# Lp-pooling on one core: a second small piece of 840 columns on partitions 30 to 89, loaded behind the first large load and stored on SP, with more implied waits declared away

## The chip, the cores and the metric

One core of one Trainium2 chip. Times are device microseconds of a whole execution of the kernel; "span" is the part of it that the profile covers, from the first to the last instruction.

A word on names. The profile counts sixteen DMA engines. A transfer over all 128 partitions is split over the sixteen (eight packets each; those of the first large load land at 19.63 to 20.34 us in the kernel before). I call one such engine with its packets a **ring**. q1 is the queue that SP issues to (all 2,432 load packets of 52,736 bytes are in it in the kernel before), q10 the one of ACT, ScalarE's sequencer (with the 896 packets of the seven ACT stores). Where both hold packets a ring takes from both: the sixteenth ran stores of 26,368 bytes and loads of 52,736 by turns from 75.04 to 86.72 us. ACT also stands for ScalarE, DVE for VectorE.

## The reference

```python
x: (32, 256, 4096) float32, p = 2.0, kernel_size = 4
for i in range(1024):
    window = np.abs(x[:, :, 4*i:4*i+4]) ** p
    result[:, :, i] = np.mean(window, axis=-1) ** (1.0 / p)
```

With p = 2 that is the root of the mean of four squares: 134.22 MB are read and 33.55 MB written, with very little arithmetic on each number.

## The kernel before

The input is treated as one flat array, 262,144 columns on 128 partitions. It is cut into 20 big loads, most of 13,184 columns (6.75 MB), which turn through three SBUF slots. For each: ScalarE squares in place, VectorE sums groups of four into an output tile, ScalarE takes the root, and the tile is stored.

```python
slots = [[(W, [W])]] * 17 + [[(W, [6592, 6592])]]                       # load widths and chunks
slots += [[(W, [5792, 7392])], [(10808, [6592, 2808, 1408])]]
ODD = 840                                                              # columns of the small piece
...
Q = 30
odd = ODD * P // Q
t = o_tiles[1][0:Q, 0:odd]                                             # 30 rows of 3,584 columns
nc.sync.dma_start(out=t, in_=...)                                      # first of all transfers
while ahead < n and loads[ahead][0] < X_SLOTS:
    load(ahead)                                                        # three big loads, on SP
    ahead += 1
nc.vector.tensor_tensor(out=t, in0=t, in1=t, op=mult)                  # the small piece: square,
nc.vector.tensor_reduce(out=o, in_=..., op=add)                        # sum,
nc.scalar.activation(out=o, in_=o, func=Sqrt, scale=1.0 / k)           # root,
stores["odd"] = nc.scalar.dma_start(...)                               # store on ACT
...
follows(ins, before)   # declares: ins needs no wait of its own on these, another wait implies it
```

Seven of the big stores are issued by ACT, the last four by SP.

Of the kernel before, what the change touches and what calls it, by code (L numbers as in the profile page):

```python
# [8 lines left out]
@with_exitstack  # L9
def kernel(  # L10
    ctx: ExitStack,
    tc: tile.TileContext,
    x: bass.AP,
    p: float,
    kernel_size: int,
    out: bass.AP,
):

    nc = tc.nc

    assert float(p) == 2.0, "kernel specialized for p == 2"
    k = int(kernel_size)
    assert k == 4, "kernel specialized for kernel_size == 4"  # L30

    P = nc.NUM_PARTITIONS
    fp32 = mybir.dt.float32
    Act = mybir.ActivationFunctionType
    xf = x.rearrange("b c l -> (b c l)")
    of = out.rearrange("b c l -> (b c l)")
    total = xf.shape[0] // P

    W, O_W = 13184, 6592
    X_SLOTS, O_SLOTS = 3, 2  # L40
    slots = [[(W, [W])]] * 17 + [[(W, [6592, 6592])]]
    slots += [[(W, [5792, 7392])], [(10808, [6592, 2808, 1408])]]
    ODD = 840
    groups = [2] * 9 + [1, 1]
    late = {7, 8, 9, 10}
    in_x = {9: (2, 0), 10: (2, 3296)}
    FINE, ENDS, LAGS = {19}, {18}, {8: 2}
    PAIRS = 15
    ON_DVE = {(18, 0)}

    loads = [(s, sum(w for w, _ in slot[:j]), *slot[j]) for s, slot in enumerate(slots)
             for j in range(len(slot))]
    n = len(loads)
    assert sum(w for _, _, w, _ in loads) + ODD == total

    firsts = [sum(groups[:g]) for g in range(len(groups))]
    assert sum(groups) == n
    group_of = [g for g, count in enumerate(groups) for _ in range(count)]
    columns = [sum(w for _, _, w, _ in loads[firsts[g]:firsts[g] + groups[g]])  # L60
               for g in range(len(groups))]

    x_pool = ctx.enter_context(tc.tile_pool(name="x_pool", bufs=1))
    o_pool = ctx.enter_context(tc.tile_pool(name="o_pool", bufs=1))

    x_tiles = [x_pool.tile([P, W], fp32, name=f"xt{j}") for j in range(X_SLOTS)]
    o_tiles = [o_pool.tile([P, O_W], fp32, name=f"ot{j}") for j in range(O_SLOTS)]
    ctx.enter_context(tc.manual_schedule())

    def block(flat, g, div):  # L70
        at, width = sum(columns[:g]) * P // div, columns[g] * P // div
        return flat[at:at + width].rearrange("(p w) -> p w", p=P)

    xs = {}
    by_load = []

    def load(i):
        s, at, w, _ = loads[i]
        v = x_tiles[s % X_SLOTS][:, at:at + w]
        g = group_of[i]  # L80
        src = sum(loads[j][2] for j in range(firsts[g], i))
        nc.sync.dma_start(out=v, in_=block(xf, g, 1)[:, src:src + w])  # L82
        xs[i] = v

    ots = {}

    stores = {}  # L90
    by_act = []
    sums = []

    def follows(ins, before):
        for b in before:
            tc.declare_no_dep(ins.ins, b.ins, reason="follows from other waits")

    def store(g, queue):
        stores[g] = queue.dma_start(out=block(of, g, k), in_=ots[g])

    def root(g, o, ends):
        r = nc.scalar.activation(out=o, in_=o, func=Act.Sqrt, scale=1.0 / k)  # L102
        follows(r, by_act[:-1] + list(stores.values()))
        by_act.append(r)
        if ends and g not in late:
            held.append(g)

    def total_sum(o, v, i):
        add = mybir.AluOpType.add
        if i < PAIRS:  # L110
            r = nc.vector.tensor_reduce(  # L111
                out=o, in_=v.rearrange("p (n j) -> p n j", j=k),
                axis=mybir.AxisListType.X, op=add,
            )
            follows(r, sums[:-1])
            sums.append(r)
            return

        q = v.rearrange("p (n j) -> p n j", j=k)
        front = v[:, 0:v.shape[1] // 2]  # L120
        h = front.rearrange("p (n j) -> p n j", j=2)
        r = nc.vector.tensor_tensor(out=h, in0=q[:, :, 0:2], in1=q[:, :, 2:4], op=add)  # L122
        follows(r, sums[:-1] + by_load)
        r = nc.vector.tensor_tensor(out=o, in0=h[:, :, 0], in1=h[:, :, 1], op=add)  # L124
        follows(r, sums[:-1])
        sums.append(r)

    Q = 30
    odd = ODD * P // Q  # L130
    t = o_tiles[1][0:Q, 0:odd]
    nc.sync.dma_start(out=t, in_=xf[(total - ODD) * P:total * P].rearrange("(p w) -> p w", p=Q))  # L132
    ahead = 0
    while ahead < n and loads[ahead][0] < X_SLOTS:
        load(ahead)
        ahead += 1
    nc.vector.tensor_tensor(out=t, in0=t, in1=t, op=mybir.AluOpType.mult)  # L137
    o = o_tiles[1][0:Q, odd:odd + odd // k]
    nc.vector.tensor_reduce(  # L139
        out=o, in_=t.rearrange("p (n j) -> p n j", j=k),  # L140
        axis=mybir.AxisListType.X, op=mybir.AluOpType.add,
    )
    nc.scalar.activation(out=o, in_=o, func=Act.Sqrt, scale=1.0 / k)  # L143
    stores["odd"] = nc.scalar.dma_start(
        out=of[(total - ODD) * P // k:total * P // k].rearrange("(p w) -> p w", p=Q), in_=o,
    )
    pending = []
    held = []
    done = 0
    for i in range(n):  # L150
        s, _, w, chunks = loads[i]
        while ahead < n and loads[ahead][0] < s + X_SLOTS:
            load(ahead)
            ahead += 1
        g = group_of[i]
        if i == firsts[g]:
            t, first = (o_tiles[g % O_SLOTS], 0) if g not in in_x else (x_tiles[in_x[g][0]], in_x[g][1])
            ots[g] = t[:, first:first + columns[g] // k]
            summed = rooted = 0
        assert sum(chunks) == w  # L160
        c = 0
        for step in chunks:
            v = xs[i][:, c:c + step]
            if (i, c) in ON_DVE:
                r = nc.vector.tensor_tensor(out=v, in0=v, in1=v, op=mybir.AluOpType.mult)  # L165
                follows(r, sums[:-1])
            else:
                r = nc.scalar.activation(out=v, in_=v, func=Act.Square)  # L168
                follows(r, by_act[:-1])
                by_act.append(r)  # L170
            total_sum(ots[g][:, summed:summed + step // k], v, i)

            while held:
                store(held.pop(), nc.scalar)
            while pending and pending[0][0] <= done - LAGS.get(pending[0][1], 1):
                root(*pending.pop(0)[1:])
            done += 1
            c += step
            summed += step // k
            ends = summed == columns[g] // k  # L180
            if ends or i in FINE or (i in ENDS and c == w):
                pending.append((done - 1, g, ots[g][:, rooted:summed], ends))
                rooted = summed
    for job in pending:
        root(*job[1:])
    for g in sorted(late):
        store(g, nc.sync)
# [35 lines left out]
```

## Time and profile before

| | before |
|---|---|
| time | 394.32 us median of three runs (394.24 to 394.44) |
| span | 392.0 us |
| traffic | 167.77 MB, 428 GB/s over the span |
| VectorE, ScalarE busy | 70%, 70% |
| last landing of a transfer | 391.21 us |
| the run that the profile shows | 393.78 us |

The lines behind this stand in the prediction below. Beside the views of the profile I use two readings of the same trace. The **packet records** give start, duration, queue and size of every DMA packet, without a ring number; a ring can be followed, because each of its packets starts where the one before ends (the load packet at 71.83 us took 3.22, and a store packet starts at 75.04). The **landings** are the sixteen increments with which a transfer reports; each is one ring's share. For the first small load in 30 rows one increment comes at 1.30 us (no ring behind it) and fifteen come with the data, at 4.30 to 4.64.

### The profile page before, as it was taken

The page shows a single profiled execution, that of the slowest core. Times are in us where ns is not written, and L with a number is a line of the kernel's source. Part 1 is how long each engine was busy: PE and PEld are TensorE (multiplying, and loading weights), DVE is VectorE, ACT ScalarE, POOL GpSimd, SP SyncE. Part 2 cuts the span into 40 slices and gives each one's busy share as a digit, 9 for nine tenths or more (in the row PEclk, how much of TensorE's full clock was granted, in tenths as well). Part 3 has the DMA queues.
Part 4 walks back from the last instruction along what each step waited for, and adds up shares of the span by engine and source line. Part 5 has one row for each costly group of instructions (what it writes and reads, how often), then busy time and mean ns, then how long its engine had stood idle before and what let it go on. Part 6 is the DMA issues. An engine that isn't in the chain of part 4 may idle for free.

```text
span 392.0 us, 183 instructions
## 1 busy us (share of the span) xinstructions
DVE 274.5 (70%) x36; ACT 275.3 (70%) x38; POOL 0.2 (0%) x4
## 2 busy tenths in 40 slices
DVE  5207898885769476948693869386939690989991
ACT  1095879909890999099909990998099809987991
POOL 0000000000000000000000000000000000000000
DMA  9899999899999999999899999999989998999997
GB/s 367 379 444 452 452 447 441 347 444 468 447 401 431 471 431 393 431 474 431 387 431 474 431 457 441 393 431 468 436 387 431 474 431 387 447 452 401 446 439 330
DMA packets 4554, 167.77 MB, mean 428 GB/s; under 512 B 526, under 2 KB 526, under 8 KB 556
## 3 DMA queue, kind: packets, MB, share of 16 engines
q1 hardware_dynamic: 3501, 144.04, 85.3%
q10 hardware_dynamic: 1053, 23.73, 14.1%
HBM read 134.22 MB, written 33.55 MB: 428 GB/s over the span
## 4 chain that ended last, share of the span: by engine, by line
DMA 56%; DVE 22%; ACT 19%; SPq 0%; issue 0%
DMA xt<-in_x_dram 56%; ACT xt L168 19%; DVE ot L111 18%; DVE xt L122 3%; DVE ot L124 1%; DVE xt L124 1%; ACT xt L102 1%; SPq L132 0%; SPq L82 0%
## 5 line engine op out<-in xcount | busy, mean ns | idle before, releaser
L168 ACT ACTIVATE xt<-xt 128x13184 f32<-128x13184 f32 (+4 forms) x23 | 217.4, 9458 | 97.0 <-DMA xt<-in_x_dram 97.0
L111 DVE TENSOR_REDUCE ot<-xt 128x3296 f32<-128x13184 f32 x15 | 208.3, 13885 | 88.0 <-ACT xt L168 88.0
L102 ACT ACTIVATE ot<-ot 128x6592 f32<-128x6592 f32 x9 | 51.1, 5680 | 0.0
L122 DVE TENSOR_TENSOR xt<-xt 128x3296 f32<-128x3296 f32 (+5 forms) x9 | 34.5, 3835 | 16.5 <-ACT xt L168 16.4
L124 DVE TENSOR_TENSOR ot<-xt 128x3296 f32<-128x3296 f32 (+1 forms) x4 | 10.9, 2733 | 0.1
L143 ACT ACTIVATE ot<-ot 30x896 f32<-30x896 f32 x1 | 0.9, 948 | 10.5 <-DVE ot L139 10.5
L124 DVE TENSOR_TENSOR xt<-xt 128x1448 f32<-128x1448 f32 (+4 forms) x5 | 7.0, 1409 | 0.2
L137 DVE TENSOR_TENSOR ot<-ot 30x3584 f32<-30x3584 f32 x1 | 3.9, 3878 | 4.7 <-DMA ot<-in_x_dram 4.7
L102 ACT ACTIVATE xt<-xt 128x3296 f32<-128x3296 f32 (+3 forms) x4 | 5.8, 1445 | 1.1 <-DVE xt L124 1.1
L165 DVE TENSOR_TENSOR xt<-xt 128x5792 f32<-128x5792 f32 x1 | 6.2, 6182 | 0.0
L139 DVE TENSOR_REDUCE ot<-ot 30x896 f32<-30x3584 f32 x1 | 3.9, 3874 | 0.0
L143 ACT ACT_TABLE_LOAD x1 | 1.3, 1283 | 0.7 <-PEq L204 0.7
L204 POOL MEMSET const-bfloat16-1.0<- 128x1 bf16 x1 | 0.1, 103 | 0.0
L204 POOL MEMSET const-uint8-127<- 128x1 uint8 x1 | 0.1, 103 | 0.0
L204 POOL MEMSET const-float32-1.0<- 128x1 f32 x1 | 0.1, 100 | 0.0
L204 POOL MEMSET const-float32-0.0<- 128x1 f32 x1 | 0.1, 99 | 0.2 <-issue 0.2
## 6 DMA issues: line engine op xcount, KB each, us to landing
xt<-in_x_dram SPq DMA_DIRECT2D x19, 6592.0 KB, 31.6
out_dram<-ot ACTq DMA_DIRECT2D x7, 3296.0 KB, 27.2
out_dram<-ot SPq DMA_DIRECT2D x2, 3296.0 KB, 23.9
xt<-in_x_dram SPq DMA_DIRECT2D x1, 5404.0 KB, 23.9
out_dram<-xt SPq DMA_DIRECT2D x1, 1648.0 KB, 11.0
out_dram<-xt SPq DMA_DIRECT2D x1, 1351.0 KB, 6.6
ot<-in_x_dram SPq DMA_DIRECT2D x1, 420.0 KB, 3.9
out_dram<-ot ACTq DMA_DIRECT2D x1, 105.0 KB, 7.1
```

The lines of the kernel that those rows point to most:

```text
L102: r = nc.scalar.activation(out=o, in_=o, func=Act.Sqrt, scale=1.0 / k)
L111: r = nc.vector.tensor_reduce(out=o, in_=v.rearrange("p (n j) -> p n j", j=k), axis=mybir.AxisListType.X, op=add,)
L122: r = nc.vector.tensor_tensor(out=h, in0=q[:, :, 0:2], in1=q[:, :, 2:4], op=add)
L124: r = nc.vector.tensor_tensor(out=o, in0=h[:, :, 0], in1=h[:, :, 1], op=add)
L137: nc.vector.tensor_tensor(out=t, in0=t, in1=t, op=mybir.AluOpType.mult)
L139: nc.vector.tensor_reduce(out=o, in_=t.rearrange("p (n j) -> p n j", j=k), axis=mybir.AxisListType.X, op=mybir.AluOpType.add,)
L143: nc.scalar.activation(out=o, in_=o, func=Act.Sqrt, scale=1.0 / k)
L165: r = nc.vector.tensor_tensor(out=v, in0=v, in1=v, op=mybir.AluOpType.mult)
L168: r = nc.scalar.activation(out=v, in_=v, func=Act.Square)
L204: nc = _bacc.Bacc("TRN2", target_bir_lowering=False, num_devices=1)
```

## The change

The intent, as I read it: give the sixteenth ring, which takes no part in the transfers of 30 and 60 rows, still less to do, and take two short pieces off the end. The 840 columns are taken from the two last big loads (420 each). The diff below is cut: left out are an output offset that follows the load widths (3,296 to 3,191) and the move of the first piece's arithmetic to a place before the loop of loads.

```diff
-    slots += [[(W, [5792, 7392])], [(10808, [6592, 2808, 1408])]]
-    ODD = 840
+    slots += [[(12764, [5372, 7392])], [(10388, [6172, 2808, 1408])]]
+    ODD, ODD2 = 840, 840
...
-        nc.sync.dma_start(out=v, in_=block(xf, g, 1)[:, src:src + w])
+        by_load.append(nc.sync.dma_start(out=v, in_=block(xf, g, 1)[:, src:src + w]))
...
+        if g not in late:
+            follows(stores[g], by_load)          # and the same for roots and pair sums
...
+        if ahead == 1:                           # behind the first large load, on SP
+            t2 = o_tiles[1][30:90, 0:ODD2 * P // 60]
+            by_load.append(nc.sync.dma_start(out=t2, in_=...rearrange("(p w) -> p w", p=60)))
+    t2 = o_tiles[1][0:90, 0:ODD2 * P // 60]      # arithmetic on rows 0 to 89
+    o2 = o_tiles[1][0:90, 4480:4480 + ODD2 * P // 60 // k]
+    nc.vector.tensor_tensor(out=t2, in0=t2, in1=t2, op=mult)
+    r = nc.vector.tensor_reduce(out=o2, in_=..., op=add)
...
+            if i == 0:
+                nc.scalar.activation(out=o2, in_=o2, func=Act.Sqrt, scale=1.0 / k)
+                stores["odd2"] = nc.sync.dma_start(out=...p=60, in_=o2[30:90, :])
```

More of the change, by code (lines that the diff above doesn't have):

```diff
@@ L41 @@
     slots = [[(W, [W])]] * 17 + [[(W, [6592, 6592])]]
-    slots += [[(W, [5792, 7392])], [(10808, [6592, 2808, 1408])]]
-    ODD = 840
+    slots += [[(12764, [5372, 7392])], [(10388, [6172, 2808, 1408])]]
+    ODD, ODD2 = 840, 840
     groups = [2] * 9 + [1, 1]
     late = {7, 8, 9, 10}
-    in_x = {9: (2, 0), 10: (2, 3296)}
+    in_x = {9: (2, 0), 10: (2, 3191)}
     FINE, ENDS, LAGS = {19}, {18}, {8: 2}
@@ L54 @@
     n = len(loads)
-    assert sum(w for _, _, w, _ in loads) + ODD == total
+    assert sum(w for _, _, w, _ in loads) + ODD + ODD2 == total
     firsts = [sum(groups[:g]) for g in range(len(groups))]
@@ L99, in store @@
         stores[g] = queue.dma_start(out=block(of, g, k), in_=ots[g])
+        if g not in late:
+            follows(stores[g], by_load)
     def root(g, o, ends):
         r = nc.scalar.activation(out=o, in_=o, func=Act.Sqrt, scale=1.0 / k)
-        follows(r, by_act[:-1] + list(stores.values()))
+        follows(r, by_act[:-1] + list(stores.values()) + by_load)
         by_act.append(r)
@@ L124, in total_sum @@
         r = nc.vector.tensor_tensor(out=o, in0=h[:, :, 0], in1=h[:, :, 1], op=add)
-        follows(r, sums[:-1])
+        follows(r, sums[:-1] + by_load)
         sums.append(r)
@@ L131 @@
     t = o_tiles[1][0:Q, 0:odd]
-    nc.sync.dma_start(out=t, in_=xf[(total - ODD) * P:total * P].rearrange("(p w) -> p w", p=Q))
-    ahead = 0
-    while ahead < n and loads[ahead][0] < X_SLOTS:
-        load(ahead)
-        ahead += 1
+    by_load.append(nc.sync.dma_start(out=t, in_=xf[(total - ODD) * P:total * P].rearrange("(p w) -> p w", p=Q)))
     nc.vector.tensor_tensor(out=t, in0=t, in1=t, op=mybir.AluOpType.mult)
@@ L146 @@
     )
+    ahead = 0
+    while ahead < n and loads[ahead][0] < X_SLOTS:
+        load(ahead)
+        ahead += 1
+        if ahead == 1:
+            at = total - ODD - ODD2
+            t2 = o_tiles[1][30:90, 0:ODD2 * P // 60]
+            by_load.append(nc.sync.dma_start(out=t2, in_=xf[at * P:(at + ODD2) * P].rearrange("(p w) -> p w", p=60)))
+    t2 = o_tiles[1][0:90, 0:ODD2 * P // 60]
+    o2 = o_tiles[1][0:90, 4480:4480 + ODD2 * P // 60 // k]
+    nc.vector.tensor_tensor(out=t2, in0=t2, in1=t2, op=mybir.AluOpType.mult)
+    r = nc.vector.tensor_reduce(
+        out=o2, in_=t2.rearrange("p (n j) -> p n j", j=k),
+        axis=mybir.AxisListType.X, op=mybir.AluOpType.add,
+    )
+    sums.append(r)
     pending = []
@@ L171 @@
             total_sum(ots[g][:, summed:summed + step // k], v, i)
+            if i == 0:
+                nc.scalar.activation(out=o2, in_=o2, func=Act.Sqrt, scale=1.0 / k)
+                stores["odd2"] = nc.sync.dma_start(
+                    out=of[at * P // k:(at + ODD2) * P // k].rearrange("(p w) -> p w", p=60), in_=o2[30:90, :],
+                )
             while held:
```

## The prediction

> **What bounds the kernel now.** I read the page's slices first, then the stretches, the chain of waits, the groups, the sync engine's waits, and last the trace's single packet records, because the diff is mostly about how transfers are dealt out. The slices give one digit per fortieth of the span:
>
> ```profile
> DVE  5207898885769476948693869386939690989991
> ACT  1095879909890999099909990998099809987991
> DMA  9899999899999999999899999999989998999997
> GB/s 367 379 444 452 452 447 441 347 444 468 447 401 431 471 431 393 431 474 431 387 431 474 431 457 441 393 431 468 436 387 431 474 431 387 447 452 401 446 439 330
> ```
>
> VectorE and ScalarE each have holes; the transfers have none from the first slice to the last. The stretches (length, busy time of DVE, ACT, POOL, clock, DMA share, GB/s) say it more exactly:
>
> ```profile
> 0.00:20.00 20.00, 7.75 (x2) 2.23 (x2) 0.20 (x4) 1.00 0.99 407
> ...
> 83.00:344.00 261.00, 183.81 (x16) 188.50 (x21) 0.00 (x0) 1.00 1.00 433
> 344.00:386.00 42.00, 37.66 (x16) 34.29 (x11) 0.00 (x0) 1.00 0.98 424
> ```
>
> So 261 us run at 433 GB/s, share 1.00, while each compute engine works about 70%. The kernel is bound by bytes: 167.77 MB at 433 GB/s is 387.5 us, and the 392.0 us span leaves 4.5 us for everything else. The packet records name most of that: the first data packet starts at 1.74 us, the last ends at 390.71, the last landing is at 391.21, and the first packets are slow.
>
> The chain of waits looks as if compute mattered at the end:
>
> ```profile
> 344.53 23.89 DMA xt<-in_x_dram
> 368.42 0.02 issue
> 368.44 5.71 ACT xt L168
> ...
> 384.07 0.50 ACT xt L102
> ```
>
> After the last load come 16.1 us of arithmetic and then the last store. But that store is issued at 384.59 and its first packets start at 386.92, the instant the 13,184-byte packets of the store ahead of it end. At the start of the kernel a load issued at 1.24 had its first packet on an idle ring at 2.83, 1.6 us later. So the last store could have begun at 386.2 and queued for 0.7 us. The arithmetic is just hidden.
>
> **Sixteen rings.** The packet records carry no ring number, but they can be followed, since one packet starts where its predecessor ended. The present small piece (30 rows of 14,336 bytes) goes to fifteen rings, two rows each; a sixteenth starts with a 52,736-byte packet at 2.83, while the fifteen start theirs between 3.26 and 3.80. The sixteen landings of each transfer show the result: the sixteenth ring lands its share of the first load at 19.63 and the others at 20.09 to 20.34, and it stays about 0.5 us ahead until its packet at 71.83, which takes 3.22 us instead of 1.95. That is when the first full-width store begins on the ACT queue, which the fifteen had already used for the small store and the sixteenth had not. From then on it is the last: the load at 355.62 has fifteen landings up to 355.32 and one at 355.62. At the end the fifteen finish their last packets at 390.14 to 390.42 and the sixteenth at 390.71. **Only these 0.29 us separate the kernel from what its other rings allow.**
>
> [...] one landing at 1.30, the other fifteen at 4.30 to 4.64. [...] the trace shows 52,736-byte loads and 26,368-byte stores alternating. [...] 14,336-byte packets took 0.58 to 1.07 us, but all in the first 3.8 us.
>
> **The change, part by part.**
>
> *Transfers.* The packet sizes give a straight line: 26,368 bytes take 978 ns and 52,736 take 1947, so 27.2 bytes per ns plus 9 ns a packet (3,584 bytes predicted 141, seen 140). The new piece gives each of fifteen rings four rows of 7,168 bytes in, 4 x 272 = 1.09 us, and four of 1,792 out, 4 x 75 = 0.30, together **+1.39 us**. The 840 columns leave the two last big loads (420 each): 8 rows x 840 x 4 bytes = 26,880 bytes a ring, 0.99 us, and a quarter of that on the way out, 0.25, together **-1.24 us** on all sixteen. So fifteen rings gain work, **+0.15 us**, and the sixteenth loses 1.24. The fifteen's last packet moves from 390.42 to 390.57, the sixteenth's from 390.71 to about 389.5. The last packet is now a fifteenth ring's, at 390.57: **-0.14 us**. No rate changes, and none of the rings is idle while work is queued.
>
> *Arithmetic.* These are the rows for the old piece, from which I scale:
>
> ```profile
> L143 ACT ACTIVATE ot<-ot 30x896 f32<-30x896 f32 x1 | 0.9, 948 | 10.5 <-DVE ot L139 10.5
> ...
> L137 DVE TENSOR_TENSOR ot<-ot 30x3584 f32<-30x3584 f32 x1 | 3.9, 3878 | 4.7 <-DMA ot<-in_x_dram 4.7
> ...
> L139 DVE TENSOR_REDUCE ot<-ot 30x896 f32<-30x3584 f32 x1 | 3.9, 3874 | 0.0
> ```
>
> Rows are 1,792 long now, so the square and the sum cost about 2.0 us each, the root of 448 about 0.57. The piece lands about 21.5; VectorE is idle there from 12.5 to 31.58, so its 4 us are free. The root stands behind the first big square, ends near 32.2, and ScalarE would otherwise wait until 35.95. Nothing is added to a path.
>
> *The store on SP.* SP issues in order, so the next load cannot go out before about 32.2; it was not due until 45.49 in any case. On the ring the store stands behind two queued loads and lands about 52; the sum that needs its columns again runs near 79.
>
> *The shift.* Loads from the second on land about 1.1 us later, and the 840 columns less at the end pay it back. Slots come free with the same margin (the load issued at 61.09 found its ring busy until 67.08).
>
> *Tail.* The last load lands near 368.46 rather than 368.42, with 420 columns less behind it: 0.36 us on the square, about 0.35 on the sums and 0.1 on the root. The last store is issued about 0.75 us earlier and waits so much longer in the queue. Worth nothing.
>
> *Waits declared away.* A wait already satisfied shows as a 17 ns semaphore event, on engines with slack. Nothing.
>
> Sum: 394.32 - 0.14 = **394.2 us**.
>
> **Rivals.**
>
> *The relief counts in full.* If the sixteenth ring held back every slot, 1.24 us would come off: 393.1. Its lag of 0.3 us at each landing speaks for it, but ring queues never run dry, so a late landing in mid-kernel delays nothing; and the fifteen stand only 0.29 us behind it at the end.
>
> *The tail is the bound.* A shorter arithmetic tail would give 0.75 us: 393.6. Against it is the queueing of 0.7 us before the last store's first packet.
>
> *The new piece disturbs its neighbours.* [...] In the slow first wave 52,736 bytes took 2.3 to 2.7 us instead of 1.95. A ring that loses 0.5 us never gets it back: 394.6 or somewhat more.
>
> *A wait takes the place.* If the new store held SP or its tile, a load would come late. The margins of 13 and 27 us above speak against it; it would show as about 1 us: 395.
>
> **Range and chances.** The first reading is worked out from measured terms, and the runs of before spread by 0.2 us; disturbance and a fuller relief are about equally likely around it. I take 393.75 to 394.65 for 8 in 10. Two per cent is 7.9 us; the span holds only 4.5 us beyond pure transfer, so faster by 2% needs less traffic, which there isn't: 0.005. Slower by 2% needs an unforeseen stall: 0.01. Within: 0.985.
>
> **What would show it.** Right: share 1.00 and 433 GB/s in mid-kernel; the new load with fifteen late landings; the sixteenth ring first, not last, by about 0.9 us at every landing from 100 us on, and the last packets of the fifteen within 0.3 us of 390.57; the last store issued near 383.9, yet starting only when the store ahead ends. Wrong: a hole in the packets of any ring, a ring other than the sixteenth alone behind the rest, or the sixteenth still last, which would mean that it loses time for another reason than its share of rows.

The landings at 1.30 and at 4.30 to 4.64 are those of the first small load. That 60 rows would go to fifteen rings was not shown by then; in the changed kernel the load in 60 rows has one increment at 2.23 us, fifteen at 21.47 to 22.16. That SP issues in order is seen in the changed kernel: it waited 29.0 us for the small store's root, issued that store at 32.38 and the next load at 45.84, as the program has them.

## The result, and the profile after

The changed kernel takes **394.25 us** median of six runs (394.13 to 394.29). In all six runs known of the kernel before by then, its median was 394.38 (393.67 to 394.98). Ratio 0.9997, 95% interval 0.9984 to 1.001: the same. A ratio here is the mean time of one kernel's runs over the mean of the other's in the same rounds, so it is not quite the ratio of the medians quoted.

The slices of the changed kernel, of which I show the two lines for the transfers:

```profile
DMA  8999999999999999999999999999999999999997
GB/s 313 430 480 430 430 436 435 430 390 470 430 430 395 465 430 427 425 438 430 430 430 430 430 435 427 454 446 422 430 465 430 401 433 473 424 416 421 420 434 336
```

No slice after the first has a hole. The first ones can't be compared with those of before by eye: these views count a packet whole where it starts (370 and 407 GB/s, or 7.40 and 8.13 MB). With its bytes spread over its time, the first 20 us moved 7.32 MB, against 7.41 before. The stretches (start and end, length, busy time of DVE, ACT, POOL, clock, DMA share, GB/s):

```profile
0.00:20.00 20.00, 7.75 (x2) 2.23 (x2) 0.20 (x4) 1.00 0.91 370
...
83.00:344.00 261.00, 184.18 (x16) 186.91 (x21) 0.00 (x0) 1.00 1.00 433
344.00:386.00 42.00, 38.03 (x16) 35.34 (x11) 0.00 (x0) 1.00 1.00 430
```

The 261 us in the middle run at 433 GB/s as before. What is new is found in the timeline (start, duration, engine, line, operation, and in brackets the idle time before and what ended it):

```profile
20.70 11.19 ACT L185 ACTIVATE xt<-xt 128x13184 f32<-128x13184 f32 x1 [7.03 <-DMA xt<-in_x_dram]
22.26 2.02 DVE L158 TENSOR_TENSOR ot<-ot 90x1792 f32<-90x1792 f32 x1 [9.57 <-DMA ot<-in_x_dram]
24.31 2.02 DVE L159 TENSOR_REDUCE ot<-ot 90x448 f32<-90x1792 f32 x1
31.80 0.56 ACT L190 ACTIVATE ot<-ot 90x448 f32<-90x448 f32 x1
31.92 13.89 DVE L114 TENSOR_REDUCE ot<-xt 128x3296 f32<-128x13184 f32 x1 [5.59 <-ACT xt L185]
32.38 0.36 SPq L191 DMA_DIRECT2D out_dram<-ot  x1
37.76 11.19 ACT L185 ACTIVATE xt<-xt 128x13184 f32<-128x13184 f32 x1 [5.41 <-DMA xt<-in_x_dram]
45.84 0.34 SPq L83 DMA_DIRECT2D xt<-in_x_dram  x1
```

The piece's square, sum and root lie in time that was idle before, and its store goes out 13 us before SP has its next load to issue. All of this arithmetic is free. At the other end, the chain of waits of the changed kernel (start, duration, what):

```profile
341.53 0.02 issue
341.56 11.29 ACT xt L185 x2
...
358.38 5.67 DVE xt L182
...
374.69 2.86 ACT xt L105
...
384.16 0.50 ACT xt L105
```

Before, the tail hung on the landing of the last load at 368.42. Now it hangs on VectorE's work from the load of 341.53, and the last root starts at 384.16 against 384.07. The shorter last loads made no earlier last store.

The landings tell of the rings. Here are sixteen landings of the load that lands near 356, and of the last store, in order of time (from the trace; the first line of each pair is the kernel before):

```
load near 356  before  355.11 355.12 355.13 ... 355.31 355.32 | 355.62
               after   354.68 | 356.02 356.07 356.10 ... 356.41 356.56 356.61
last store     before  390.71 390.79 390.82 ... 391.06 391.07 | 391.21
               after   389.63 | 390.91 390.99 391.00 ... 391.19 | 391.39 391.42 391.44
```

The sixteenth ring, last before, is now 1.3 us ahead of all others. And yet the last landing has moved from 391.21 to **391.44**, since the fifteen finish later. Finally, what SP does after the last landing. These are the groups of the kernel's closing line, before and after; the three numbers are the shortest, median and longest duration in ns, then the first and last start:

```profile
L218 SPq EVENT_SEMAPHORE  x6: 17/28/3252, 385.0 to 391.9; - x6
```

```profile
L240 SPq EVENT_SEMAPHORE  x6: 17/28/6333, 385.1 to 392.3; - x6
```

Both kernels close with six waits on SP, mostly on two semaphores each. Before, the long wait, in which the last store lands, began at 387.98 and was the last of those on transfers. After, it begins at 385.12, and two waits, on transfers long done, still stand behind it, each with 64 ns from one start to the next. From the last landing to the end of the span it takes 0.79 us before and 0.92 after.

### The profile page after: what moved, and what is told of

The parts are those of the page before. It is cut to its first block, busy times and chain, and to the rows that moved or that the text cites. A ratio compares the mean times of both kernels' runs of the same rounds, so it can differ in the third digit from the quotient of the medians.

```text
span 392.4 us, 186 instructions
## 1 busy us (share of the span) xinstructions
DVE 277.4 (71%) x38; ACT 275.2 (70%) x39; POOL 0.2 (0%) x4
## 4 chain that ended last, share of the span: by engine, by line
DMA 50%; DVE 24%; ACT 22%; another core or an unknown queue 1%; SPq 0%; issue 0%
DMA xt<-in_x_dram 50%; ACT xt L185 21%; DVE ot L114 18%; DVE xt L125 3%; DVE xt L182 1%; ACT xt L105 1%; DVE xt L127 1%; DVE ot L127 0%; SPq L135 0%; SPq L154 0%; SPq L83 0%
## 5 line engine op out<-in xcount | busy, mean ns | idle before, releaser
L185 ACT ACTIVATE xt<-xt 128x13184 f32<-128x13184 f32 (+5 forms) x23 | 217.1, 9443 | 96.8 <-DMA xt<-in_x_dram 96.8
L125 DVE TENSOR_TENSOR xt<-xt 128x6592 f32<-128x6592 f32 (+6 forms) x9 | 34.1, 3786 | 16.2 <-ACT xt L185 16.0
L158 DVE TENSOR_TENSOR ot<-ot 90x1792 f32<-90x1792 f32 x1 | 2.0, 2022 | 9.6 <-DMA ot<-in_x_dram 9.6
L127 DVE TENSOR_TENSOR xt<-xt 128x1343 f32<-128x1343 f32 (+4 forms) x5 | 6.8, 1365 | 0.2
L105 ACT ACTIVATE xt<-xt 128x3191 f32<-128x3191 f32 (+3 forms) x4 | 5.6, 1406 | 1.2 <-DVE xt L127 1.2
L182 DVE TENSOR_TENSOR xt<-xt 128x5372 f32<-128x5372 f32 x1 | 5.7, 5748 | 0.0
L159 DVE TENSOR_REDUCE ot<-ot 90x448 f32<-90x1792 f32 x1 | 2.0, 2016 | 0.0
```

The source lines that it names most:

```text
L105: r = nc.scalar.activation(out=o, in_=o, func=Act.Sqrt, scale=1.0 / k)
L125: r = nc.vector.tensor_tensor(out=h, in0=q[:, :, 0:2], in1=q[:, :, 2:4], op=add)
L127: r = nc.vector.tensor_tensor(out=o, in0=h[:, :, 0], in1=h[:, :, 1], op=add)
L158: nc.vector.tensor_tensor(out=t2, in0=t2, in1=t2, op=mybir.AluOpType.mult)
L159: r = nc.vector.tensor_reduce(out=o2, in_=t2.rearrange("p (n j) -> p n j", j=k), axis=mybir.AxisListType.X, op=mybir.AluOpType.add,)
L182: r = nc.vector.tensor_tensor(out=v, in0=v, in1=v, op=mybir.AluOpType.mult)
```

## The experiments

Two theories at the start. **Bytes theory**: rings never run dry, the ring that has most to do ends the kernel, so only the sixteenth's small lag could be won. Rivals: full relief of the sixteenth counts; the tail of arithmetic is the bound; the new piece disturbs its neighbours; the declarations save something.

### The changed kernel again

No edit.

> The changed kernel once more, for five rounds beside the kernel before. Bytes theory: 0.1 to 0.2 us below the kernel before (ratio 0.9995 to 0.9998, not clear of noise); the sixteenth ring lands its share of the last store 1.0 to 1.6 us ahead of the other fifteen. Full-relief rival: 1.2 us below (0.997). Disturbance rival: 0.3 us or more above (1.001).

Measured 394.25 us (394.06 to 394.46) against 394.16 for the kernel before, ratio 1.0002 (0.9989 to 1.0014). The sixteenth ring leads by 1.6 us at the last store (389.48 against 391.05); the last landing is 391.76, and fourteen of the fifteen have landed by 391.56. Full relief is out: the sixteenth is relieved, and nothing came off (1.2 us would be a ratio of 0.997).

### The second piece on all sixteen rings

```diff
-  t2 = o_tiles[1][30:90, ...]   # 60 rows of 1,792 columns
+  t2 = o_tiles[1][30:94, ...]   # 64 rows of 1,680 columns
```

> The changed kernel with the second piece cut into 64 rows instead of 60, so that it goes to all sixteen rings: same bytes, same place, no relief for the sixteenth. Bytes theory: each ring carries what it did in the kernel before plus 8 packet costs of 9 ns, so the fifteen end 0.1 us earlier than in the changed kernel and the sixteenth is last again, by about 0.3 us, as before the change; time within 0.2 us of both. If relief of the sixteenth were worth its full 1.24 us, this run would lose all of it and be 1.2 us above the changed kernel.

Measured 394.30 (394.06 to 394.52), ratio 1.0005 (0.9991 to 1.0018). As expected the time is that of both. The sixteen land the last store within 390.86 to 391.36. No ring is set apart at the end, as it should be if the 64 rows went to all sixteen; the sixteenth led by 0.4 us until the first large store, then lost the lead. So its expected lag of 0.3 did not appear; taking its relief away cost nothing.

### The second piece on seven rings: an overdose

```diff
-  t2 = o_tiles[1][30:90, ...]   # 60 rows of 1,792 columns
+  t2 = o_tiles[1][30:65, ...]   # 35 rows of 3,072 columns
```

> The changed kernel with the second piece cut into 35 rows, so that it goes to seven rings of sixteen, five rows each: an overdose of the imbalance. Bytes theory (the busiest ring sets the end): 5 x 0.46 us in and 5 x 0.12 us out = 2.91 us on seven rings against 1.24 taken away, so these end at 390.42 + 1.67 = 392.1 against the last end of 390.71 in the kernel before: 1.4 us slower than before, 1.5 slower than the changed kernel. If only the total of the bytes counted, or if the tail of arithmetic were the bound: no change, within 0.2 us.

Measured **399.14 us** (398.72 to 399.66), ratio 1.0127 (1.0113 to 1.014): 5.0 us slower, with the same bytes in total. It did go to seven rings. The version without a small piece has 496 packets under 512 bytes, sixteen for each of its 31 transfers; the kernel before has 526, so the piece in 30 rows adds fifteen each way; this run has 540, seven each way more. The direction is that of the bytes theory, the size over three times what the bytes give. The stretches of its last 8 us:

```profile
389.00:394.00 5.00, 0.00 (x0) 0.42 (x1) 0.00 (x0) 1.00 0.76 319
394.00:397.00 3.00, 0.00 (x0) 0.00 (x0) 0.00 (x0) 1.00 0.04 17
```

From 394 on the DMA share is 0.04: two rings alone still work. The landings of the second load, in order, run from 36.01 and 36.66 to 40.45 and 41.31; and no later load has a spread under 4.3 us. So a ring that falls behind in the first 26 us **never gets it back** as long as all have work (at the last store, for which the others had to wait, 2.3 us are left). The excess is in the packet records: packets of 12,288 bytes, worth 0.46 us, took up to 1.53, and one load packet beside them took 4.37 us instead of 1.95. What made the excess is not shown. A guess that it was the place of the rows led to the next run.

### The second piece on partitions 64 to 123

```diff
-  t2 = o_tiles[1][30:90, ...]
+  t2 = o_tiles[1][64:124, ...]  # same 60 rows, arithmetic on rows 64 to 123
```

> The changed kernel with the second piece on partitions 64 to 123 instead of 30 to 89: same 60 rows, same fifteen rings[...]. [...] the 7,168-byte packets of the piece take about 0.5 us instead of 0.27, its landings come 1 to 2 us later than 21.5 to 22.2[...], and the kernel ends 1 to 2 us later than the changed kernel. [...] packets of 0.27 us, and the same time within 0.2 us.

The first figures are for a place that counts, an estimate, and the last for one that doesn't.

Measured 395.11 us (394.94 to 395.13), ratio 1.0025 (1.001 to 1.004). The median packet of the piece took 0.508 us, with 7,168 bytes, where the changed kernel has 0.272; the fifteen landings of the piece come at 22.36 to 22.79 instead of 21.47 to 22.16; and the last store's fifteen end at 391.89 to 392.24 instead of 390.91 to 391.44. So 0.6 to 0.9 us lost at 22 us are 0.8 to 1.0 us at the end. The place counts, and of the two partitions 30 to 89 are the better; why is not shown. The piece is not quite free there either: in the changed kernel the piece's packets take 0.311 us on average, not 0.272, with two at 0.51 and 0.54, and two rings land it at 22.02 and 22.16, after the rest had by 21.80.

### The declarations alone

```diff
+  by_load.append(...)                  # all loads
+  follows(stores[g], by_load)          # and in roots and pair sums
```

> The kernel before with the added declarations alone, without the second piece. Built, it differs from the kernel before in two instructions: VectorE's pair sums of the last two slots lose a wait on a transfer that another wait already implies. Bytes theory: nothing, within 0.2 us of the kernel before; the last of the sixteen landings at the end within 0.2 us of 391.2. A rival that credits the declarations would have it faster by at least 0.3 us.

Measured 394.21 us (393.84 to 395.08) against 394.21, ratio 1.0006 (0.9991 to 1.0021). As built, two waits of VectorE are gone and nothing else. No effect shows; the interval leaves room for 0.4 us down and 0.8 us up.

### The tail of arithmetic, lengthened twice

```diff
-  (10808, [6592, 2808, 1408])
+  (10808, [6592, 2108, 2108])          # first run
+  (10808, [6592, 1408, 2808])          # second run
```

> The kernel before with the last load's two small chunks made equal (2,108 and 2,108 columns instead of 2,808 and 1,408): same transfers, the last store issued about 0.5 us later, near 385.1. Bytes theory: hidden in the 0.7 us that this store queues for in any case; the last packets end as before, 390.7 within 0.2 us. Tail rival: 0.5 us slower.

> The kernel before with the last load's two small chunks swapped (1,408 and then 2,808 columns): same transfers, the last store issued about 2.6 us later, near 387.2. Bytes theory: 0.7 us of that are hidden and 1.9 show as a hole in the packets before the last store, so the kernel is 1.9 us slower. Tail rival: all 2.6 us show.

First run: 394.04 us (393.74 to 394.51), ratio 0.9996 (0.9979 to 1.0013). Hidden, as expected, in the median. In the profiled run, the slowest of the four, a ring that lagged by 0.9 us delayed the last load, and the last store was issued at 386.60, not at 385.1. There fifteen rings stood idle for about 0.4 us; only the lagging one, which ended the kernel, went from the store ahead to the last without a break. Second run: 394.17, 394.25, 395.80 and 395.97, ratio 1.0024 (1.0001 to 1.0048). Here the hole is to be seen. The stretches around it, first the kernel before, then the second run:

```profile
385.00:387.00 2.00, 0.00 (x0) 0.00 (x0) 0.00 (x0) 1.00 1.01 432
387.00:389.40 2.40, 0.00 (x0) 0.00 (x0) 0.00 (x0) 1.00 1.01 428
```

```profile
385.00:387.00 2.00, 1.70 (x2) 0.62 (x2) 0.00 (x0) 1.00 0.97 415
387.00:389.40 2.40, 0.81 (x1) 0.79 (x1) 0.00 (x0) 1.00 0.06 22
```

Share 0.06 where it was 1.01. In this run a ring that lagged by 1.6 us had delayed the last load, and with it the whole tail, so that the last store went out at 388.66. Its first packet started at 389.49, **0.83 us** after the issue; in the first run it was 386.60 and 387.44, 0.84 us. In the kernel before, the store issued at 384.59 could therefore have begun at 385.4, and it waited 1.5 us in the queue until 386.92, twice the 0.7 that I had worked out. Neither theory had the second run's two values apart; two of its four runs are hardly slower than the kernel before, which fits a tail that starts early when no ring lags: from the last load's landing to the last of all it took 23.5 us here, so an estimate for a last load at 368.29, where its other fifteen rings had landed, is 394.3. I did not profile those.

### The first piece on all sixteen rings

```diff
-    Q = 30
+    Q = 32
```

> The kernel before with its first small piece cut into 32 rows instead of 30, so that it goes to all sixteen rings. Two theories of why the sixteenth ring was last in the kernel before. First use: it alone met the ACT queue for the first time in a large store and lost about 1 us there; then with 32 rows all sixteen meet it in the small store, and no ring lags by more than 0.15 us behind the next at the end; 0.2 us faster than before. Slower ring: it loses that time whatever it was given first; then it lags by 0.9 to 1.1 us at the end, and the kernel is about 0.6 us slower than before.

Measured 393.76 us (393.64 to 393.97) against 394.16, ratio 0.999 (0.9978 to 1.0003). No ring stood apart after the first store, which fits 32 rows on all sixteen rings; the last landing was 0.24 us behind the next. It looked like a version that beats both, so I ran it again.

> The kernel before with its first piece in 32 rows, as in e6_first32, in new rounds. There it was 0.4 us below the kernel before, within noise. Expected again: 0.3 to 0.5 us faster, all runs between 393.5 and 394.0, no ring more than 0.3 us behind the next one; the kernel before spreads over 0.6 us or more in the same rounds because its sixteenth ring loses a varying time.

The second time it took 394.27 us (393.70 to 394.69), ratio 1.0005 (0.9992 to 1.0018): **a miss**. Two of the five were below 393.9, three at 394.27 and above. In the profiled run, the sixteen were within 0.4 us of each other up to the load of 145 us; by 369 one was 1.4 us behind (fifteen landings from 367.83 to 368.03, one at 369.38), and it ended the kernel at 392.12 against 391.01 for the next. So a single ring can lose more than a microsecond in mid-kernel although it has no more to do than the others. As the sixteen begin alike here, the records do not say which.

### Where a ring loses its time

Three runs for the cause, all on the kernel before.

```diff
-    stores["odd"] = nc.scalar.dma_start(...)
+    stores["odd"] = nc.sync.dma_start(...)
```

> The kernel before with the store of its small piece issued on SP instead of ACT: still 30 rows and fifteen rings, but no ring has used the ACT queue before the first large store. First-use theory: all sixteen lose about alike there, so the sixteenth keeps its lead of about 0.5 us over the others to the end, while all end up to 1 us later than before. If the sixteenth ring loses time because it runs ahead or for another reason of its own: it alone drops back at that store and is last, as in the kernel before, and the time is the same.

```diff
-    Q = 30
+    Q = 128
```

> The kernel before with its first piece in 128 rows of 840 columns: all sixteen rings[...]. [...] the first big packets start near 3.3 us instead of 3.3 to 4.1, the first load lands at 20.0 instead of 20.5, and the kernel is 0.2 to 0.5 us faster than with 32 rows, 0.5 to 0.9 faster than before. [...] the same as with 32 rows, within 0.2 us.

The first figures are estimates for a start slowed by the place of the 30 rows, as the piece on partitions 64 to 123 was (0.51 us a packet); the last are for a start that is slow with any rows.

```diff
-    ODD = 840; ... [(10808, [6592, 2808, 1408])]
+    no small piece; [(11648, [7432, 2808, 1408])]
```

> The kernel before without any small piece: its 840 columns go to the first chunk of the last load. All sixteen rings then begin level and meet the ACT queue for the first time in the first large store. First-use theory: all sixteen lose 0.4 to 1.3 us there, so the landings shift together between the loads of 88 and 106 us, by about 0.7 us against the kernel before, and the kernel is up to 0.7 us slower. If the loss belongs to one ring alone: one ring lags by 0.5 to 1.5 us after that store, the others do not shift. The arithmetic tail grows by 1.3 us, of which nearly all should be hidden.

With the small store on SP: 394.55 us (393.79 to 395.27), ratio 1.0015 (1.0002 to 1.0027). In the profile the sixteenth ring's packet at 71.87 took 3.09 us instead of 1.95; no other packet there lost more than 0.5. The first-use theory expected all sixteen to lose there; it **falls**. But the sixteenth was not last: it ended with the rest, its last packet at 390.63. The ring that ended the kernel, 1.3 us behind the next, was one of the fifteen; it lost 0.49 us at 70.75 and 0.81 at 149.21. The tail's second run shows the same: its lagging ring lost 0.70 us at 70.81 and 0.65 at 149.75, while the sixteenth lost 1.06 at 71.90 and ran with the rest. So the rival, a loss that belongs to the sixteenth alone, falls too.

With 128 rows: 394.70 us (393.98 to 395.08), ratio 1.0016 (1.0004 to 1.0028). The start is indeed quicker, with the first load landed at 20.07 (20.79 and 20.52 in the two runs with 32 rows): 0.5 to 0.7 us, but it is one profile, and its packets are smaller too, so the cause is not shown. Profiles with 30 rows lie between, at 20.32 to 20.71. But at 70 us, at the first large store, packets of all sixteen rings took 0.4 to 1.0 us too long, although all had used the ACT queue before. That speaks against first use once more, and it ate the gain.

Without a small piece: 395.07 us (394.78 to 395.27), ratio 1.0028 (1.0016 to 1.004). All sixteen lose 0.4 to 1.2 us in the packets that run at 70 to 72 us, as the first-use theory wanted, and the last store went out at 387.12, so the longer tail was not hidden either.

Here is the time lost in slow packets in each profile, summed over the sixteen rings: for every packet of a usual size after 30 us, its duration beyond the usual one for that size, where that is more than about 0.03 us. The run on seven rings, with 20.1, is left out. In the larger sums much of it falls at 70 to 74 us, when the first large store begins; in the second run with 32 rows, no packet lost more than 0.25 us there.

```
first piece in 32 rows      0.0      32 rows, again     1.8
piece on rows 64 to 123     0.0      tail, two runs     3.8  2.9
second piece in 64 rows     0.7      small store on SP  4.2
changed kernel, two runs    1.1 1.0  kernel before      6.3
declarations alone          2.4      no piece, 128 rows 16.5 17.2
```

It is not constant even for one kernel, and neither of my theories orders this list. One pattern stands in it: at 68 to 75 us all five profiles with the second piece lost 0.0 to 1.5 us in sum, the five with the first piece alone in 30 rows 1.9 to 6.2. No run was made to test it. **What makes a ring lose time when the first large store begins, and later, stays open.**

## Why the prediction was right or wrong

The number was right: 394.25 against 394.2, inside the range, and "the same" as forecast. That it came so close is luck. The range of 0.9 us holds the kernel before as well, so it can't tell the readings apart. And the sum takes 0.14 from a median of 394.32, while its terms come from the profile of a run of 393.78; from profile to profile the change costs 0.35 and 0.68 us.

**What bounds the kernel: right.** Share 1.00 at 433 GB/s in the middle. The profiled times follow the last landing, which is nearly given, since the kernel ends by waiting for its stores; what the table adds is how far the last ring is behind the next. It has eight of the fourteen profiled runs (in the other six the last column is 2.57 to 2.70):

| run | fifteenth landing | last landing | time | time less last landing |
|---|---|---|---|---|
| before | 391.07 | 391.21 | 393.78 | 2.57 |
| declarations alone | 390.95 | 391.26 | 393.84 | 2.58 |
| 32 rows | 391.15 | 391.39 | 393.97 | 2.58 |
| 32 rows, again | 391.01 | 392.12 | 394.69 | 2.57 |
| small store on SP | 391.12 | 392.44 | 395.02 | 2.58 |
| changed | 391.42 | 391.44 | 394.13 | 2.69 |
| changed, again | 391.56 | 391.76 | 394.46 | 2.70 |
| second piece in 64 rows | 391.35 | 391.36 | 394.06 | 2.70 |

**The gain of 0.14 us: this step failed, though bytes per ring was the right mechanism; one reading was wrong, and three terms were mis-sized or missing.** The reading: "the fifteen finish their last packets at 390.14 to 390.42" holds for fourteen; one ends at 390.55. So 0.16 us, not 0.29, stood between the sixteenth and the next (0.14 by the landings), and the prediction's own sum, 390.55 + 0.15 = 390.70 against 390.71, gives no gain at all.

The terms: (1) "Only these 0.29 us separate the kernel from what its other rings allow" also took one profile's lag for a constant. By the landings of the table the last ring of kernels without the second piece is 0.14 to 1.32 us behind the next. (2) "fifteen rings gain work, +0.15 us" was too small. The fifteenth landing is at 390.95 to 391.15 without the second piece, and at 391.42 and 391.56 with it on fifteen rings: about 0.3 to 0.6 later, from two profiles. The piece's packets at 0.311 instead of 0.272 us explain 4 x 0.04 = 0.16 on average; the two rings that landed the piece last lost some 0.25 more. Three of the fifteen ended their packets at 390.92 to 390.94, outside the 0.3 us around 390.57. The rest looks like start-up: the first load, which goes ahead of the piece, has its last landing at 20.68 and 20.67 in the two profiles of the changed kernel, at 20.34 before, but also at 20.60 with the declarations alone. The second load landed 1.8 us later than before, not 1.1. Counted in bytes, the kernel before had moved 17.81 MB by 44 us, the changed kernel 17.63 and 17.56; by 83 us it was 34.54 against 34.51 and 34.45, which matches the 6.3 us that the rings of before lost in sum at their first large store. (3) The closing waits on SP, 0.13 us, were not in the sum at all; the last column shows them.

**What the change did to the spread.** Over all rounds, the kernel before ran 33 times, from 393.67 to 394.98, median 394.15; the changed kernel eleven times, from 394.06 to 394.46, median 394.25. These are runs of several rounds, not all on the same chip. The standard deviation is 0.31 us before and 0.11 after. With only the six runs of before that stand beside the result and the nine beside the second run of the changed kernel, it is 0.35 before (median 394.24) and 0.11 after. The slow end is gone, and the fast end with it. Why is not shown. A ring far behind the next makes slow times, as the table has it, and the sixteenth, which leads now, can't be that ring any more. But in the slow profiles with the small store on SP and of the tail's second run it was another ring; and the version in 64 rows, where nothing is relieved, spread over 394.06 to 394.52, little more than the changed kernel beside it (394.06 to 394.46). In one profile of the changed kernel the sixteenth ring again lost 0.4 us in its packets at 71.86 and at 87.87, and still led by 1.3 us at the end.

**The sixteenth ring first by 0.9 us: right in kind, low in size**, 1.3 and 1.6. It lost less at the first large store than in the profile of before.

**The new load and its arithmetic: right.** Fifteen late landings at 21.47 to 22.16, 2.02 and 2.02 us on VectorE, 0.56 on ScalarE, store landed by 53.6, no load late.

**"The last store is issued about 0.75 us earlier": wrong**, 384.68 against 384.59. The step that failed: I moved only the last load. But the loads of 340 and 355 us came 1.5 and 1.0 us later, because the second piece goes ahead of them and only the last two loads are shorter. VectorE, which has to work off these two, took over the tail. It cost nothing, since the store still queued for the other rings.

**"Queued for 0.7 us": mis-sized**, it is 1.5. I had taken the latency of 1.6 us from the start of the kernel; on an idle ring late in the kernel it was 0.83 in two runs.

**Disturbance: real, in the wrong chance.** I gave it the same weight as a fuller relief. Slow packets of the piece explain a part of the +0.3 to 0.6 (0.311 us on average instead of 0.272); on partitions 64 to 123 the same piece costs 0.9 us against the kernel before, as the changed kernel does not, and on seven rings 4.9 against the changed kernel of the same rounds.

**Declarations: right.** Nothing to be seen. (A slip on which nothing rests: the first wave's packets of 52,736 bytes took 2.15 to 2.67 us, not 2.3 to 2.7.)

## What to carry to other kernels

When the transfers are never idle, look at the sixteen landings of each transfer and at the last packets: here the ring that ended last was the bound, and a ring that lost time early never got it back while all had work (a spread of 4.3 us or more at every load after the overdose). Shifting work between rings could then win no more than the distance between the last and the next, and that distance has to be read from several profiles, since one profile's value may be chance. A change of a few tenths of a microsecond needs the spread of the runs beside their median: here the median did not move while the spread fell to a third. And when a ring is called the last, follow it through the packets: the one that leads at the start and the one that ends the kernel need not be the same.
